# Seven half products in place of eight in the second feed-forward of a hybrid encoder

## The chip, the cores and the metric

The kernel runs on one core of one Trainium2 chip. The metric is the device time of one launch in microseconds (us); the comparison of two kernels uses medians of several runs on the same chip. Engines are named as the profile names them: PE is TensorE (matmuls), PEld the weight loads of TensorE, DVE is VectorE, ACT is ScalarE, POOL is GpSimd and SP issues the DMAs.

## What is computed

The reference is a two-layer encoder trunk on 512 tokens of width 1024, in float32. Each layer is a feed-forward, a mixer of four head groups, and a second feed-forward, each with an RMS norm before it. Only the second feed-forward is changed:

```
def rms_norm(x, gain):
    y = x * rsqrt(mean(x * x, axis=-1) + 1e-6)
    return y * gain

def swiglu(x, w_in, w_out):                 # w_in: 1024 x 5632, w_out: 2816 x 1024
    gate, up = split(x @ w_in, 2, axis=-1)
    return (silu(gate) * up) @ w_out

for layer in range(2):
    x = x + 0.5 * swiglu(rms_norm(x, ffn1_norm[layer]), ffn1_w_in[layer], ffn1_w_out[layer])
    x = x + hybrid_mixer(rms_norm(x, mix_norm[layer]), ...)
    x = x + 0.5 * swiglu(rms_norm(x, ffn2_norm[layer]), ffn2_w_in[layer], ffn2_w_out[layer])
```

## The kernel before

**Layout.** Everything is held transposed: x is eight tiles of 128 features by 512 tokens (x[0] to x[7]). Float32 products are formed from two parts of each operand in the type fp32r: the high part is the operand cast to fp32r, the low part is what the cast left. `mm3` (L106 to L109) issues three matmuls for one 128x128 weight block: low weight by high token (L107), high by low (L108), high by high (L109). The token operand (`norm_chunk`, L178) is x times the norm's gain, split into hh (ACT, L185) and hl (DVE, L186); the reciprocal root of the mean square, R, comes later from `norm_square` (L189; ACT squares, POOL adds, L196) and `stats` (L198), and is multiplied in behind the product.

**Weights.** `load` (L111) fetches a block of up to 128x1024 into one of two wr buffers by a DMA on SP's queue. `weights` (L116) cuts it into pieces of up to 512 columns and splits each: the cast to wh on ACT (L125), the subtraction to wl on DVE (L126). There are four wh and four wl buffers.

**The feed-forward** (`ffn`, L215). The 2816 hidden features are 22 chunks of 128, taken in four quarters of 6, 6, 5 and 5 chunks (`QS`). A chunk f loads its gate block and its up block (128x1024 each), and forms two products into two PSUM banks, pgp and pup: 8 blocks x 3 matmuls of 512 tokens each, 48 matmuls a chunk. Behind them come: gate by R (DVE, L250), Silu (ACT, L251), again by R (DVE, L252), up by gate (DVE, L254), and the split of the result (ACT, L256; DVE, L257) into `a`, of which a quarter keeps all its chunks. In chunk 0 the two products advance block by block as the norm's pieces arrive, and `stats` follows. After a quarter's chunks, `part` (L265) multiplies by the output weights: for each of 8 feature blocks d, n chunks x 3 matmuls of 512 tokens into pop (the first two blocks begin with all chunks but the last); then x[d] gets half of it added (DVE, L280), and in the last quarter the next norm's pieces are made.

**Order.** Nothing is ordered by hand here. The framework puts the instructions of each engine into one fixed order from the order in which the program writes them (earlier is more urgent), its own estimates of durations and the buffers that are free: 15 tiles of the tag t2 (128x512), 14 of k4 (128x1024), 5 of s8 (128x2048), 8 PSUM banks (three mm, two sc, two tp, one ot). At run time each engine takes its instructions in that order and waits on semaphores.

## Time and profile before

| what | us |
|---|---|
| median of 3 runs (lowest to highest) | 2024.93 (2024.31 to 2025.15) |
| the profiled execution's own time | 2025.69 |
| span in its profile, first to last instruction | 2023.9 |
| PE busy | 1969.1 |
| DVE busy | 1240.6 |
| ACT busy | 804.4 |
| POOL busy | 368.4 |

The profile's page has busy times, the chain of work that ended last (followed back from the last instruction to what released each step), groups of instructions by line, and DMA issues. The trace answers questions on a stretch of the span: busy time of each engine in it, who waited for whom, and the instructions in order of time. A matmul's recorded duration includes its way through the array, and matmuls overlap; what one costs in a row of them is the distance of their starts. The same holds, by less, on DVE and ACT. Layer 0's second feed-forward lies from about 648 us (its first matmuls run among the mixer's last) to 1025 us, layer 1's from about 1652 us to the end.

### The profile page before, as it was taken

The page shows a single profiled execution, that of the slowest core. Times are in us where ns is not written, and L with a number is a line of the kernel's source. Part 1 is how long each engine was busy: PE and PEld are TensorE (multiplying, and loading weights), DVE is VectorE, ACT ScalarE, POOL GpSimd, SP SyncE. Part 2 cuts the span into 40 slices and gives each one's busy share as a digit, 9 for nine tenths or more (in the row PEclk, how much of TensorE's full clock was granted, in tenths as well). Part 3 has the DMA queues.
Part 4 walks back from the last instruction along what each step waited for, and adds up shares of the span by engine and source line. Part 5 has one row for each costly group of instructions (what it writes and reads, how often), then busy time and mean ns, then how long its engine had stood idle before and what let it go on. Part 6 is the DMA issues. An engine that isn't in the chain of part 4 may idle for free.

```text
span 2023.9 us, 26161 instructions
## 1 busy us (share of the span) xinstructions
PE 1969.1 (97%) x9768; PEld 1648.9 (81%) x9768; DVE 1240.6 (61%) x2327; ACT 804.4 (40%) x1523; POOL 368.4 (18%) x349
## 2 busy tenths in 40 slices
PE   8999999998999999999999999999989989999999
PEld 6788878897977788888888888888978778888887
DVE  6865547657887545444577655465687875444454
ACT  4333323444676323233442333334547653232332
POOL 4010100254445000000120101002544540000000
PEclk9999999998999999999999999999989999999999
DMA  5232343331312332323233332423313122333233
GB/s 176 82 104 88 104 83 106 97 114 51 97 55 72 97 101 91 97 89 109 84 116 88 102 93 93 102 88 103 119 39 99 50 66 94 99 96 103 81 107 104
DMA packets 74447, 189.24 MB, mean 93 GB/s; under 512 B 16960, under 2 KB 22848, under 8 KB 74320
## 3 DMA queue, kind: packets, MB, share of 16 engines
q1 hardware_dynamic: 74224, 187.51, 30.7%
q8 instruction: 76, 1.25, 0.3%
q14 instruction: 51, 0.42, 0.1%
q0 software_dynamic: 96, 0.07, 0.0%
HBM read 182.86 MB, written 4.69 MB: 93 GB/s over the span
## 4 chain that ended last, share of the span: by engine, by line
PE 83%; DVE 10%; ACT 4%; issue 2%; POOL 1%; DMA 0%; SPq 0%; DVEq 0%; ACTq 0%; POOLq 0%
PE pop L109 9%; PE pop L108 9%; PE pop L107 9%; PE pup L107 7%; PE pgp L107 7%; PE pgp L108 7%; PE pgp L109 7%; PE pup L109 7%; PE pup L108 7%; PE ppr L107 1%; PE ppr L108 1%; PE ppr L109 1%; DVE wl L126 1%; PE pfp L448 1%; DVE hl L186 1%
## 5 line engine op out<-in xcount | busy, mean ns | idle before, releaser
L125 ACT CAST wh<-wr 128x512 fp32r<-128x512 f32 (+2 forms) x718 | 405.9, 570 | 962.8 <-PE pgp L109 314.0
L126 DVE TENSOR_TENSOR wl<-wr,wh 128x512 fp32r<-128x512 f32 (+2 forms) x618 | 409.4, 665 | 380.0 <-ACT wh L125 378.3
L107 PE MATMUL pgp<-hh,wl 128*128 128x512 f32 x704 | 275.5, 391 | 7.6 <-DVE wl L126 7.6
L107 PE MATMUL pup<-hh,wl 128*128 128x512 f32 x704 | 276.3, 392 | 3.2 <-DVE wl L126 3.2
L107 PE MATMUL pop<-a,wl 128*128 128x512 f32 x704 | 277.0, 395 | 1.4 <-DVE wl L126 1.4
L108 PE MATMUL pgp<-hl,wh 128*128 128x512 f32 x704 | 275.5, 391 | 2.4 <-DVE hl L186 2.4
L109 PE MATMUL pop<-a,wh 128*128 128x512 f32 x704 | 276.3, 392 | 0.0
L108 PE MATMUL pop<-a,wh 128*128 128x512 f32 x704 | 274.5, 390 | 0.6 <-DVE a L257 0.6
L108 PE MATMUL pup<-hl,wh 128*128 128x512 f32 x704 | 275.0, 391 | 0.0
L109 PE MATMUL pup<-hh,wh 128*128 128x512 f32 x704 | 275.0, 391 | 0.0
L109 PE MATMUL pgp<-hh,wh 128*128 128x512 f32 x704 | 274.7, 390 | 0.0
L196 POOL TENSOR_TENSOR t<-t,sq 128x512 f32<-128x512 f32 x42 | 60.0, 1430 | 664.9 <-ACT sq L195 663.6
L107 PEld LDWEIGHTS pgp<-hh,wl 128*128 128x128 f32 x704 | 132.6, 188 | 35.7 <-DVE wl L126 8.0
L126 POOL TENSOR_TENSOR wl<-wr,wh 128x512 fp32r<-128x512 f32 (+1 forms) x100 | 131.2, 1317 | 161.7 <-ACT wh L125 125.4
L107 PEld LDWEIGHTS pup<-hh,wl 128*128 128x128 f32 x704 | 132.5, 188 | 33.6 <-DVE wl L126 5.6
L108 PEld LDWEIGHTS pgp<-hl,wh 128*128 128x128 f32 x704 | 132.6, 188 | 32.9 <-DVE hl L186 5.5
L109 PEld LDWEIGHTS pop<-a,wh 128*128 128x128 f32 x704 | 132.2, 188 | 30.6
L108 PEld LDWEIGHTS pop<-a,wh 128*128 128x128 f32 x704 | 132.2, 188 | 30.2 <-DVE a L257 1.0
L107 PEld LDWEIGHTS pop<-a,wl 128*128 128x128 f32 x704 | 132.3, 188 | 28.9 <-DVE wl L126 2.1
L109 PEld LDWEIGHTS pup<-hh,wh 128*128 128x128 f32 x704 | 132.4, 188 | 27.6
L109 PEld LDWEIGHTS pgp<-hh,wh 128*128 128x128 f32 x704 | 132.4, 188 | 27.6
L108 PEld LDWEIGHTS pup<-hl,wh 128*128 128x128 f32 x704 | 132.5, 188 | 27.4
(263 smaller groups left out, 3071.3 us busy)
## 6 DMA issues: line engine op xcount, KB each, us to landing
wr<-in_f_w SPq DMA_DIRECT2D x176, 512.0 KB, 3.4
wr<-in_f_w SPq DMA_DIRECT2D x64, 384.0 KB, 3.1
wr<-in_f_w SPq DMA_DIRECT2D x64, 320.0 KB, 2.9
wr<-in_wm SPq DMA_DIRECT2D x36, 512.0 KB, 3.5
bias<-in_ctab SPq DMA_DIRECT2D x8, 448.0 KB, 3.4
bias<-in_rbx SPq DMA_DIRECT2D x8, 448.0 KB, 3.8
wr<-in_woC SPq DMA_DIRECT2D x8, 384.0 KB, 3.1
x<-in_xt SPq DMA_DIRECT2D x8, 256.0 KB, 6.4
```

The costliest lines, as they stand in the source:

```text
L107: nc.tensor.matmul(out, ll, rh, start=start, stop=False)
L108: nc.tensor.matmul(out, lh, rl, start=False, stop=False)
L109: nc.tensor.matmul(out, lh, rh, start=False, stop=stop)
L125: nc.scalar.copy(hi[:, :w], r)
L126: (nc.gpsimd if pooled else nc.vector).tensor_tensor(lo[:, :w], r, f32(hi[:, :w]), op=ALU.subtract)
L186: stt(hl, x[c], gcol, f32(hh), op0=ALU.mult, op1=ALU.subtract)
L196: gtt(acc, acc, sq, op=ALU.add)
L448: nc.tensor.matmul(pt[r0:r0 + 64, c0 + 16:c0 + 144], bm[q][:, g].rearrange("p a c -> p (a c)"), v[q][:, g].rearrange("p j c -> p (j c)"), ...
```

## The change

The second feed-forward of both layers is called with `fast=True`; in it, chunks 1 to 21 take a new path, chunk 0 the old one. Of each chunk the gate weights (ga) and the up weights (ua) are cut into two halves of the input features, and the tokens into two halves of 256 (HT); the 2x2 product of halves is then formed from seven products of a half weight (128 outputs by 512 inputs) with a half token set, each 4 blocks x 3 matmuls of 256 tokens (`product`), 84 matmuls a chunk.

- **Weights:** four sums of weight halves, s1 to s4, are formed on POOL; then seven operands (a11, s1, a12, a22, s2, s4, s3) are each split by `split` (ACT cast, DVE subtraction, 512 columns). ga still goes through `load`; ua is loaded into a k4 tile.
- **Tokens:** `token_forms` makes, once per call, four combinations of token halves for each of the four pairs of feature tiles: two products with the gain on ACT, two differences of 256 columns on POOL, two on DVE, then a split of 1024 columns (ACT cast, DVE subtraction) into an s8 tile kept for the whole call.
- **Results:** products are gathered in the banks px, pz, py and pv; ACT copies four halves of 256 columns out of PSUM (c1, c2), DVE adds four halves of 256 columns, one input in PSUM, into g (gate) and u (up).
- **Order:** the seventh product (s3, `finish`) and all that follows it are put off: `close` of a chunk is issued in the middle of the next chunk, after its second product; that of a quarter's last chunk between the output products' first two parts. In `close` the second multiplication by R is on POOL.

```diff
--- before.py
+++ after.py
@@ -212,16 +212,115 @@
         nc.scalar.copy(R, rp)
         return R, rc, ms
 
-    def ffn(l, which, next_norm, hooks):
+    def split(src):
+        hi = pool.tile([P, 512], F32R, tag="wh", bufs=4, name=nm("wh"))
+        lo = pool.tile([P, 512], F32R, tag="wl", bufs=4, name=nm("wl"))
+        nc.scalar.copy(hi, src)
+        tt(lo, src, f32(hi), op=ALU.subtract)
+        return hi, lo
+
+    HT = S // 2
+
+    def token_forms(idx):
+        out = []
+        for kp in range(KC // 2):
+            ha, hb = t2(name="ha"), t2(name="hb")
+            act(ha, x[kp], AF.Copy, scale=gains[:, idx, kp:kp + 1])
+            act(hb, x[kp + 4], AF.Copy, scale=gains[:, idx, kp + 4:kp + 5])
+            s = k4([P, 4, HT], name="tsum")
+            gtt(s[:, 0], ha[:, HT:], ha[:, :HT], op=ALU.subtract)
+            gtt(s[:, 2], hb[:, HT:], ha[:, HT:], op=ALU.subtract)
+            tt(s[:, 1], hb[:, HT:], s[:, 0], op=ALU.subtract)
+            tt(s[:, 3], hb[:, :HT], s[:, 1], op=ALU.subtract)
+            tf = s8([P, 2, 4, HT], F32R, name="tf")
+            nc.scalar.copy(tf[:, 0], s)
+            tt(tf[:, 1], s, f32(tf[:, 0]), op=ALU.subtract)
+            out.append(tf)
+        return out
+
+    def product(out, w, right, first, last):
+        for kp in range(KC // 2):
+            lhs = [a[:, kp * P:(kp + 1) * P] for a in w]
+            rh, rl = right(kp)
+            nc.tensor.matmul(out, lhs[1], rh, start=first and kp == 0, stop=False, skip_group_check=True)
+            nc.tensor.matmul(out, lhs[0], rl, start=False, stop=False, skip_group_check=True)
+            nc.tensor.matmul(out, lhs[0], rh, start=False, stop=last and kp == KC // 2 - 1, skip_group_check=True)
+
+    def ffn(l, which, next_norm, hooks, fast=False):
         w1 = t["f%d_w1" % which]
         w2 = t["f%d_w2" % which]
+        forms = []
+
+        def part_of(half, lo):
+            return lambda kp: (h[kp + 4 * half][0][:, lo:lo + HT], h[kp + 4 * half][1][:, lo:lo + HT])
+
+        def form(i):
+            return lambda kp: (forms[kp][:, 0, i], forms[kp][:, 1, i])
+
+        def begin(f, before):
+            ga = load(w1[l, f, 0], 1024)
+            ua = k4([P, 1024], name="ua")
+            nc.sync.dma_start(ua, w1[l, f, 1])
+            a11, a12, a21, a22 = ga[:, :512], ga[:, 512:], ua[:, :512], ua[:, 512:]
+            s1, s2, s3, s4 = t2(name="s1"), t2(name="s2"), t2(name="s3"), t2(name="s4")
+            gtt(s1, a21, a22, op=ALU.add)
+            gtt(s2, s1, a11, op=ALU.subtract)
+            gtt(s4, a12, s2, op=ALU.subtract)
+            gtt(s3, a11, a21, op=ALU.subtract)
+            px, pz = bank("sc", name="px"), bank("tp", name="pz")
+            product(px[:, :HT], split(a11), part_of(0, 0), True, True)
+            c1, c2 = t2(name="c1"), t2(name="c2")
+            nc.scalar.copy(c1[:, :HT], px[:, :HT])
+            product(pz[:, :HT], split(s1), form(0), True, True)
+            nc.scalar.copy(c2[:, :HT], pz[:, :HT])
+            if before is not None:
+                before()
+            py = bank("mm", name="py")
+            product(py[:, :HT], split(a12), part_of(1, 0), True, True)
+            pv = bank("mm", name="pv")
+            product(pv[:, :HT], split(a22), form(3), True, True)
+            g, u = t2(name="g"), t2(name="u")
+            tt(g[:, :HT], c1[:, :HT], py[:, :HT], op=ALU.add)
+            nc.scalar.copy(c2[:, HT:], pv[:, :HT])
+            product(px[:, :HT], split(s2), form(1), False, True)
+            nc.scalar.copy(c1[:, HT:], px[:, :HT])
+            product(pz[:, :HT], split(s4), part_of(1, HT), False, True)
+            tt(g[:, HT:], c1[:, HT:], pz[:, :HT], op=ALU.add)
+
+            def finish():
+                product(px[:, :HT], split(s3), form(2), False, True)
+                tt(u[:, :HT], px[:, :HT], c2[:, HT:], op=ALU.add)
+                tt(u[:, HT:], px[:, :HT], c2[:, :HT], op=ALU.add)
+
+            return g, u, finish
         if l == 0 and which == 1:
             norm_chunk(0, 0)
         h = state["h"]
+        norm_idx = 3 * l + (0 if which == 1 else 2)
         R = None
         for qi, (f0, f1) in enumerate(QS):
             av = []
+            pend = None
+
+            def close(g, u, finish):
+                finish()
+                tt(g, g, R, op=ALU.mult)
+                act(g, g, AF.Silu)
+                gtt(g, g, R, op=ALU.mult)
+                af = t2(name="af")
+                tt(af, u, g, op=ALU.mult)
+                a = k4([P, 2, S], F32R, name="a")
+                nc.scalar.copy(a[:, 0], af)
+                tt(a[:, 1], af, f32(a[:, 0]), op=ALU.subtract)
+                av.append(a)
+
             for f in range(f0, f1):
+                if fast and f >= 1:
+                    if not forms:
+                        forms += token_forms(norm_idx)
+                    before = None if pend is None else (lambda p=pend: close(*p))
+                    pend = begin(f, before)
+                    continue
                 pre = early if f == 0 else []
                 gw = weights(w1[l, f, 0], 1024, raw=pre.pop(0) if pre else None)
                 uw = weights(w1[l, f, 1], 1024, raw=pre.pop(0) if pre else None)
@@ -270,6 +369,8 @@
                     mm3(ops[d], *ws[d](i * P), av[i][:, 0], av[i][:, 1], i == 0, i == n - 1)
 
             part(0, range(n - 1))
+            if pend is not None:
+                close(*pend)
             part(1, range(n - 1))
             for d in range(KC):
                 if d < 2:
@@ -944,7 +1045,7 @@
             for _ in hooks:
                 pass
         mixer(l, T, 3 * l + 2)
-        ffn(l, 2, 3 * l + 3 if l + 1 < DEPTH else None, None)
+        ffn(l, 2, 3 * l + 3 if l + 1 < DEPTH else None, None, True)
 
 
 def _tables():
```

## Rows read from the trace of the kernel before

**Rows 1.** page, busy time of the engines and the chain that ended last

```profile
PE 1969.1 (97%) x9768; PEld 1648.9 (81%) x9768; DVE 1240.6 (61%) x2327; ACT 804.4 (40%) x1523; POOL 368.4 (18%) x349
...
PE 83%; DVE 10%; ACT 4%; issue 2%; POOL 1%; DMA 0%; SPq 0%; DVEq 0%; ACTq 0%; POOLq 0%
```

**Rows 2.** windows over layer 0's second feed-forward, columns in the first row

```profile
core 0: us, PE busy (x) PEld busy (x) DVE busy (x) ACT busy (x) POOL busy (x), PEclk, DMA share, GB/s
...
668.00:1025.00 357.00, 357.00 (x1574) 294.55 (x1574) 181.82 (x279) 122.36 (x212) 10.14 (x8) 1.00 0.31 96
690.00:721.00 31.00, 31.00 (x139) 25.66 (x138) 14.74 (x23) 9.83 (x17) 0.00 (x0) 1.00 0.29 90
721.00:754.00 33.00, 33.00 (x146) 27.07 (x145) 14.78 (x25) 9.16 (x17) 0.00 (x0) 1.00 0.35 102
```

**Rows 3.** waits in 668 to 1025 us (total us, times, longest)

```profile
DVE wl L126 <- ACT wh L125: 96.2, 75, 2.9
...
ACT wh L125 <- PE pgp L109: 74.5, 40, 2.9
```

**Rows 4.** DVE timeline (start us, us, instruction): after two up products

```profile
688.84 0.69 DVE L254 TENSOR_TENSOR af<-pup,sg 128x512 f32<-128x512 f32 x1 [1.39 <-PE pup L109]
...
699.72 0.69 DVE L254 TENSOR_TENSOR af<-pup,sg 128x512 f32<-128x512 f32 x1 [1.39 <-PE pup L109]
```

**Rows 5.** PE timeline in the mixer, first and last of 19 matmuls

```profile
460.22 0.28 PE L109 MATMUL ppr<-wh,hh 128*128 128x256 f32 x1
...
462.38 0.28 PE L109 MATMUL ppr<-wh,hh 128*128 128x256 f32 x1
```

**Rows 6.** DVE timeline, two operations back to back

```profile
680.53 0.68 DVE L257 TENSOR_TENSOR a<-af,a 128x512 fp32r<-128x512 f32 x1
...
681.13 0.68 DVE L252 TENSOR_TENSOR sg<-sg,R 128x512 f32<-128x512 f32 x1
```

**Rows 7.** groups by form, all of the span: busy us, mean ns, idle before

```profile
L815 POOL TENSOR_TENSOR zi<-zi,rot 128x512 f32<-128x512 f32 x4 | 5.2, 1292 | 9.2 <-DVE zi L812 9.2
...
L716 DVE TENSOR_TENSOR pT<-ptp,pT 128x256 fp32r<-128x256 f32 x32 | 12.5, 416 | 3.0 <-ACT pT L715 3.0
...
L405 DVE TENSOR_TENSOR k<-k,k 128x1024 f32<-128x1024 f32 x4 | 4.9, 1215 | 0.0
...
L125 ACT CAST wh<-wr 128x512 fp32r<-128x512 f32 x446 | 275.0, 620 | 621.2 <-PE pgp L109 254.1 <-PE pup L109 225.3 <-PE pop L109 76.0
```

**Rows 8.** POOL and DVE timelines at a norm's square, both idle before

```profile
1013.75 1.29 POOL L196 TENSOR_TENSOR t<-t,sq 128x512 f32<-128x512 f32 x1 [2.44 <-ACT sq L195]
...
1014.14 1.45 DVE L126 TENSOR_TENSOR wl<-wr,wh 128x512 fp32r<-128x512 f32 x1 [0.28 <-ACT wh L125]
1015.51 0.68 DVE L280 SCALAR_TENSOR_TENSOR x<-pop,x 128x512 f32<-128x512 f32 x1
```

**Rows 9.** POOL and DVE timelines where both have work queued

```profile
650.85 9.93 POOL L196 TENSOR_TENSOR t<-t,sq 128x512 f32<-128x512 f32 x6 [0.42 <-ACT sq L195]
...
654.32 1.27 DVE L759 TENSOR_TENSOR x<-pop,x 128x512 f32<-128x512 f32 x2
...
655.52 4.13 DVE L186 SCALAR_TENSOR_TENSOR hl<-x,gains,hh 128x512 fp32r<-128x512 f32 x3
```

**Rows 10.** DVE and PE timelines early in layer 0's second feed-forward

```profile
662.59 1.28 DVE L126 TENSOR_TENSOR wl<-wr,wh 128x512 fp32r<-128x512 f32 x2
...
668.47 0.49 PE L108 MATMUL pgp<-hl,wh 128*128 128x512 f32 x1
```

**Rows 11.** PE timeline and windows after an idle stretch in the mixer

```profile
491.90 0.69 PE L849 MATMUL pyp<-zi,s 128*128 128x64 f32 x2 [5.67 <-DVE zi L837]
...
495.00:500.00 5.00, 5.00 (x25) 4.92 (x25) 2.23 (x4) 2.55 (x5) 0.00 (x0) 0.50 0.00 0
500.00:505.00 5.00, 5.00 (x25) 5.00 (x24) 2.03 (x3) 3.07 (x5) 0.00 (x0) 0.50 0.00 0
505.00:510.00 5.00, 5.00 (x43) 5.00 (x42) 4.52 (x12) 3.47 (x9) 1.31 (x1) 0.95 0.02 3
```


## The prediction

> **What bounds the kernel now.** I read the busy times and the chain that ended last first: TensorE is busy 97% of the span and holds 83% of the chain, VectorE 61% of the span, GpSimd 18% [rows 1]. But the change acts in one stage, so I read the windows over that stage: in layer 0's second feed-forward PE is busy 357.00 of 357 us at the full granted clock (1.00), DVE 181.82, GpSimd 10.14 and, between the norms, 0.00 [rows 2]. The waits of the stage say the same: ScalarE waits for matmuls to free a weight buffer, VectorE for ScalarE, and neither holds PE up [rows 3]. So the stage is a row of matmuls, and its price is their number by the distance of their starts. Two successive chunks end their up product 699.72 - 688.84 = 10.88 us apart [rows 4]: 48 matmuls of 512 tokens, 0.227 us each.
>
> **What the change takes from PE.** 42 chunks (21 in each of two layers) get 84 matmuls of 256 tokens in place of 48 of 512. The mixer has such a row: 18 distances in 462.38 - 460.22 = 2.16 us, 0.120 us each, every one with a weight block of its own [rows 5]. A chunk then costs 84 x 0.120 = 10.08 us, and PE saves 0.80 x 42 = 33.6 us. That is 7%, not an eighth: 0.120 is more than half of 0.227, because part of a matmul's price does not shrink with its tokens. The Trainium skill ("TensorE: Matmul & The Clock Gate", Back-to-back issue gap) gives N/2.4 + 2.5 ns for a lone matmul, 109 and 216 ns here; by it a chunk would save some 1.2 us and the change 50 us, an estimate that the rows, with 120 and 227 ns, do not bear out.
>
> **What it adds elsewhere.** A chunk's work off PE, with the distance of two DVE operations of 512 columns, 681.13 - 680.53 = 0.60 us [rows 6], and the durations of [rows 7]:
> - POOL: four sums of weight halves and one multiplication by R, five of 512 columns at 1.29 us alone, 6.5 us; before it had none here.
> - DVE, both inputs in SBUF: seven weight subtractions in place of four, g by R, u by g, the low part of a: 10 x 0.60 = 6.0 us.
> - DVE, one input in PSUM: four sums of 256 columns, at most 0.42 us each (the price of such a one), 1.7 us.
> - ACT: seven casts at 0.62, Silu and the cast of a at about the same, and four half-width copies at no more: under 8.1 us of 10.08, hidden beside PE. If it were not, a late cast would hold its product up.
> - DMA: the same bytes in as many transfers on SP's queue; ua goes to a k4 tile, so the wr pair turns over half as often. I cost it at nothing; DMA's share is 0.29 in the chunks now [rows 2].
>
> Each of these sums is under 10.08 us, so PE would stay the bound if they ran side by side. They do not. Where POOL adds a square and DVE meets a subtraction with both inputs in SBUF, that subtraction takes 1.45 us and ends after the POOL operation [rows 8], against 0.68 [rows 6]. Where both queues are full, six POOL operations take 9.93 us, 1.655 each, and the DVE operations beside them 4.13/3 = 1.38 each; two DVE operations that read a PSUM bank, issued in the same stretch, take 1.27 together, undisturbed [rows 9]. So the two take turns, a POOL operation keeping DVE out for about 1.655 - 0.60 = 1.05 us. One chunk then needs 5 x 1.05 + 6.0 = 11.25 us of turns, plus the PSUM sums where they don't fall into POOL's turns: between 0 and 1.7, and I take a quarter of it, 0.4, because POOL's pairs fill about three quarters of the time (5 x 1.655 of 11.25). **11.65 us a chunk**, 11.25 to 12.9, against 10.08 on PE and 10.88 before. While it lasts, this makes a chunk slower, by 0.77.
>
> **What covers it.** The excess of 1.57 us falls only on a chunk in which the one before is closed and the next one's sums are made. A quarter's first chunk closes none, its last prepares none, and the output products (33 us with DVE busy 14.78 and POOL idle [rows 2]) let the next quarter begin with four operands split: three products ahead of PE, 3 x 12 x 0.120 = 4.3 us.
> - Quarter of six: 4 x 1.57 - 4.3 = 2.0 us of stall. Quarters of five: 3 x 1.57 - 4.3 = 0.4 each.
> - First quarter: chunk 1 also needs the token forms. For four pairs that is 2 POOL differences (half of 1.05 each), 2 DVE differences (0.42) and a DVE subtraction of 1024 columns (1.22): 4 x 3.11 = 12.4 us of turns, with chunk 1's four sums (4.2) and two splits (1.2) 17.8 us. DVE is free for it at 662.59 + 1.28 = 663.9, PE begins chunk 1 at 668.47 [rows 10] and can do three products (4.3 us) without the last form, to 672.8. If all 17.8 come first, PE waits until 681.7, 8.9 us; if POOL's part hides wholly, 4 x 2.06 + 1.2 = 9.4 us end at 673.3 and it waits 0.5. I take 6, nearer the upper end, because [rows 9] shows the two queues interlocked in just this stretch. Then chunks 2 to 4 with a lead of two products: 3 x 1.57 - 2.9 = 1.8.
> - The close of a quarter's last chunk (two PSUM sums, three operations of 0.6 to 0.7 on DVE, ACT, DVE: some 2.6 us) lies under 12 to 15 output matmuls of 0.227: 2.7 to 3.4 us. Nothing, with no room to spare.
>
> **Sum.** Per layer 6 + 1.8 + 2.0 + 0.4 + 0.4 = 10.6 us of stall, 21.2 in all: 33.6 - 21.2 = 12.4 us gained. The profiled execution took 2025.69 by itself (span 2023.9), 0.8 above the median; 2025.69 - 12.4 = 2013.3, and against the median **2012.5 us**.
>
> **Rivals.**
> - **The turns bind in every chunk** (slower). Place: DVE's queue in chunks 1 to 21. DVE's order is fixed and POOL takes its turn whenever its next tiles are free, so the lead of three products may be gone at once and never come back. It decides if products wait for wl from a quarter's second chunk on. Price: (11.65 - 10.88) x 42 = 32 us and 12 for the forms: 2024.9 + 44 = 2069; with half of it 2047, with 12.9 a chunk some 2120. For it: [rows 8, 9]. Against it: the tiles for the next chunk's sums come free only as operands are split, which holds POOL back. The Trainium skill has this as a rule ("SBUF — State Buffer", Who interferes with whom): a VectorE instruction with two SBUF inputs and a GpSimd one that reads SBUF exclude each other for the whole instruction. The trace agrees that one waits; taken strictly with 1.29 and 0.60 it would be 12.45 us a chunk, where six turns show 1.655 us and not 1.89 a pair. Chance 0.27.
> - **The forms cost the clock** (about no change). An idle stretch of 5.67 us in the mixer was followed by matmuls at a granted clock of 0.50, the 1.2 GHz level, until about 505 us [rows 11], some 13 us, half of them lost. If chunk 1 waits that long in one piece, each layer loses some 6.5 more: 2012.5 + 13 = 2026, 2019 to 2035. Against it: the forms come in four pieces, with matmuls between. Chance 0.25.
> - **All cover holds**: forms done within chunk 0, no excess: 2024.9 - 33.6 + 3 = 1994. It asks that POOL and DVE meet seldom; [rows 9] speaks against that. Chance 0.07.
> - That matmuls of 256 tokens don't save what they should (0.130 each would end it: 84 x 0.130 = 10.9) I leave out; [rows 5] has the same shape with new weights each time.
>
> **How the numbers follow.** The forecast has 0.41 (2001 to 2021). No change means within 0.2%, 4 us, about what a measurement of this kernel can tell: 2020.9 to 2029. Faster: 0.41 + 0.07 + 0.02 of the clock case = 0.50. Same: 0.15 of the clock case. Slower: 0.08 of the clock case and 0.27 = 0.35. The low end, 1999, leaves out nearly all of the cover case; the high end, 2056, the upper half of the first rival. Faster cases hold half, with a range of their own of 1994 to 2020.
>
> **What would show it.** PE: 84 matmuls of 256 tokens at 0.120 where nothing stalls. DVE over 85% busy in the chunks; POOL's sums at about 1.7 us instead of 1.29; DVE subtractions at about 1.4 beside them. PE idle for wl by a few us in chunk 1 of each layer, by one or two in the later chunks of a quarter, hardly in the last. It is wrong if such waits come in every chunk (first rival), if the granted clock falls in chunk 1 (second), or if chunks of 10.1 us follow each other from the start (third).

## The result and the profile after

The changed kernel takes **2130.81 us** (2127.08 to 2139.25, four runs) where the kernel before takes 2025.04 on the same chip: a ratio of 1.0528, interval 1.0497 to 1.056. It is 106 us slower. The forecast was 2012.5, and even the range, which ended at 2056, missed it. The profiled execution below is the longest of the four (2139.25 us, span 2137.5).

The page after, busy times, chain, and two of the costliest groups:

```profile
PE 1980.6 (93%) x11280; PEld 1731.8 (81%) x11280; DVE 1504.2 (70%) x2603; ACT 937.5 (44%) x1841; POOL 713.3 (33%) x575
...
PE 74%; DVE 17%; ACT 4%; issue 4%; POOL 1%; DMA 0%; SPq 0%; DVEq 0%; ACTq 0%; POOLq 0%
...
L219 DVE TENSOR_TENSOR wl<-s,wh 128x512 fp32r<-128x512 f32 x168 | 179.7, 1081 | 49.0 <-ACT wh L218 48.9
...
L245 PE MATMUL ppz<-tf,wl 128*128 128x256 f32 x168 | 59.0, 351 | 96.0 <-DVE wl L219 96.0
```

Against [rows 1], PE has fallen from 97% to 93% of a longer span, and DVE's share of the chain has risen from 10% to 17%. PE now stands idle 96 us ahead of one group of matmuls, those of the second product (bank pz, left operand s1), and each time VectorE's subtraction for s1 is what it waits for. The subtractions for the four sums take 1.081 us each on the mean, where operations of the same size took 0.68 [rows 6].

The windows over layer 0's second feed-forward (columns: stretch, length, busy time and count of PE, PEld, DVE, ACT and POOL, granted PE clock, DMA share, GB/s), with the stretch of chunk 1 in pieces:

```profile
668.00:1060.00 392.00, 343.07 (x2243) 319.11 (x2242) 298.22 (x399) 180.21 (x355) 174.99 (x115) 0.92 0.26 80
665.00:670.00 5.00, 2.24 (x15) 1.71 (x14) 0.85 (x2) 1.58 (x2) 1.03 (x1) 0.76 0.36 148
670.00:675.00 5.00, 2.69 (x12) 2.40 (x12) 3.96 (x5) 4.99 (x9) 3.38 (x5) 0.50 0.00 0
...
690.00:695.00 5.00, 2.82 (x13) 2.82 (x14) 5.00 (x5) 0.00 (x0) 3.27 (x2) 0.50 0.03 4
695.00:700.00 5.00, 5.00 (x32) 5.00 (x32) 1.82 (x4) 2.04 (x5) 0.00 (x0) 0.67 0.30 104
```

Where [rows 2] had PE busy 357 of 357 us at clock 1.00, it is now busy 343 of 392 at 0.92. Two separate losses show: one long hole in chunk 1 with the clock at 0.50 (the 1.2 GHz level) on both sides of it, and many small ones later. The waits of the stage name three causes (total us, times, longest; the last row is of the queue on which SP issues DMAs):

```profile
POOL s L266 <- DMA ua<-in_f_w: 78.6, 16, 7.0
...
PE ppz L245 <- DVE wl L219: 47.4, 14, 19.5
...
ACT R L212 <- PE prp L210: 10.8, 1, 10.8
```

```profile
SPq L113 <- DVE wl L219: 259.3, 21, 31.5
...
SPq L263 <- PE ppx L247: 0.3, 1, 0.3
```

**Chunk 1.** The timelines of ACT, POOL, DVE and PE there, in this order (start, us, instruction, idle before it and what ended it):

```profile
668.40 0.58 ACT L212 COPY R<-prp 128x512 f32<-128x512 f32 x1 [10.76 <-PE prp L210]
...
670.83 0.71 ACT L228 ACTIVATE ha<-x,gains 128x512 f32<-128x512 f32 x1
...
671.62 0.73 POOL L231 TENSOR_TENSOR tsum<-ha 128x256 f32<-128x256 f32 x1 [4.28 <-ACT ha L228]
...
683.73 6.72 DVE L237 TENSOR_TENSOR tf<-tsum,tf 128x1024 fp32r<-128x1024 f32 x3
690.38 1.74 DVE L219 TENSOR_TENSOR wl<-s,wh 128x512 fp32r<-128x512 f32 x1
...
692.18 0.58 PE L245 MATMUL ppz<-tf,wl 128*128 128x256 f32 x1 [19.49 <-DVE wl L219]
```

ACT stood idle for 10.76 us although the forms' inputs were there: its queue held the copy of R first, and R waits for the statistics. So the forms began at 670.8 and not at 663.9. From then on VectorE and GpSimd were in each other's way; a 1024-column subtraction took 6.72/3 = 2.24 us (1.215 in [rows 7]), and all four stood in VectorE's queue ahead of s1's subtraction, for which the second product waits.

PE's row, before and then after, shows smaller losses on both sides of the hole (pst is the bank of the statistics' first matmuls, for the mean squares; a second group spreads what R is copied from):

```profile
665.39 0.39 PE L107 MATMUL pgp<-hh,wl 128*128 128x512 f32 x1
...
667.66 0.95 PE L203 MATMUL pst<-ones,t 128*128 128x2 f32 x8
```

```profile
665.09 0.95 PE L203 MATMUL pst<-ones,t 128*128 128x2 f32 x8
...
669.76 0.58 PE L245 MATMUL ppx<-hh,wl 128*128 128x256 f32 x1 [1.40 <-DVE sg L349]
...
698.32 0.29 PE L246 MATMUL ppv<-tf,wh 128*128 128x256 f32 x1
```

Before, chunk 1's gate product started at 665.39 us, and its matmuls filled PE's time around the statistics, whose two groups of matmuls took PE 0.81 and 0.35 us by the distance of starts. In the change chunk 1's first product needs a bank that comes free only behind R, and 669.76 - 665.09 = 4.67 us pass from the statistics to it: 3.5 us more. When it starts, the matmuls run at half clock already: its eleven distances, to 672.28 us, take 2.52 us, 1.2 more than at 0.119 (a chunk of e10, below, divided by 84). The hole is 19.90 us from start to start, 19.8 more than one distance, and the 28 distances behind it, up to 698.32 us, take 6.14 us, 2.8 more. Together chunk 1 loses 27.3 us here, 4.0 of them by the clock.

**The later chunks.** SP, POOL, DVE and PE around the second product of one chunk:

```profile
718.16 0.33 SPq L113 DMA_DIRECT2D wr<-in_f_w  x1
718.54 0.43 SPq L263 DMA_DIRECT2D ua<-in_f_w  x1
731.62 0.33 SPq L113 DMA_DIRECT2D wr<-in_f_w  x1
...
723.25 1.31 POOL L266 TENSOR_TENSOR s<-ua 128x512 f32<-128x512 f32 x1 [6.31 <-DMA ua<-in_f_w]
...
729.79 1.77 DVE L219 TENSOR_TENSOR wl<-wr,wh 128x512 fp32r<-128x512 f32 x1
...
728.22 0.39 PE L245 MATMUL ppz<-tf,wl 128*128 128x256 f32 x1 [1.89 <-DVE wl L219]
741.54 0.38 PE L245 MATMUL ppz<-tf,wl 128*128 128x256 f32 x1 [1.55 <-DVE wl L219]
```

This is a loop. SP issues a gate load into a wr buffer as soon as VectorE has subtracted the gate half that stood there (729.79 + 1.77 = 731.56, issue at 731.62), and the up load ua only behind it. ua lands 4.7 us after its issue (718.54 to 723.25), POOL forms s1 from it, ACT casts it, VectorE subtracts, PE runs, and VectorE's next subtraction of a gate half frees the next buffer. These two chunks follow each other 741.54 - 728.22 = 13.32 us apart, where the kernel before had 10.88 [rows 4].

### The profile page after: what moved, and what is told of

It reads as the page before. It is cut to its first block, busy times and chain, and to the rows that moved or that the text cites. A ratio compares the mean times of both kernels' runs of the same rounds, so it can differ in the third digit from the quotient of the medians.

```text
span 2137.5 us, 30236 instructions
## 1 busy us (share of the span) xinstructions
PE 1980.6 (93%) x11280; PEld 1731.8 (81%) x11280; DVE 1504.2 (70%) x2603; ACT 937.5 (44%) x1841; POOL 713.3 (33%) x575
## 3 DMA queue, kind: packets, MB, share of 16 engines
q8 instruction: 88, 1.44, 0.3%
## 4 chain that ended last, share of the span: by engine, by line
PE 74%; DVE 17%; ACT 4%; issue 4%; POOL 1%; DMA 0%; SPq 0%; DVEq 0%; ACTq 0%; POOLq 0%
PE pop L108 8%; PE pop L109 8%; PE pop L107 8%; DVE wl L219 3%; PE pup L107 3%; PE pgp L107 3%; PE pgp L109 3%; PE pgp L108 3%; PE pup L108 3%; PE pup L109 3%; PE ppz L245 2%; PE ppx L245 2%; PE ppx L246 2%; PE ppx L247 2%; PE ppz L247 2%
## 5 line engine op out<-in xcount | busy, mean ns | idle before, releaser
L219 DVE TENSOR_TENSOR wl<-s,wh 128x512 fp32r<-128x512 f32 x168 | 179.7, 1081 | 49.0 <-ACT wh L218 48.9
L107 PE MATMUL pgp<-hh,wl 128*128 128x512 f32 x368 | 144.6, 393 | 7.9 <-DVE wl L126 7.8
L107 PE MATMUL pup<-hh,wl 128*128 128x512 f32 x368 | 145.7, 396 | 3.4 <-DVE wl L126 3.4
L108 PE MATMUL pgp<-hl,wh 128*128 128x512 f32 x368 | 144.8, 393 | 2.4 <-DVE hl L186 2.4
L108 PE MATMUL pup<-hl,wh 128*128 128x512 f32 x368 | 144.3, 392 | 0.0
L109 PE MATMUL pup<-hh,wh 128*128 128x512 f32 x368 | 144.1, 392 | 0.0
L109 PE MATMUL pgp<-hh,wh 128*128 128x512 f32 x368 | 144.0, 391 | 0.0
L107 PE MATMUL ppr<-wh,hl 128*128 128x256 f32 x448 | 127.8, 289 | 1.4 <-ACT q L666 1.4
L108 PE MATMUL ppr<-wl,hh 128*128 128x256 f32 x448 | 127.8, 286 | 0.7 <-POOL wl L126 0.7
L109 PE MATMUL ppr<-wh,hh 128*128 128x256 f32 x448 | 127.6, 286 | 0.0
```

Source lines behind the costliest of these rows:

```text
L107: nc.tensor.matmul(out, ll, rh, start=start, stop=False)
L108: nc.tensor.matmul(out, lh, rl, start=False, stop=False)
L109: nc.tensor.matmul(out, lh, rh, start=False, stop=stop)
L219: tt(lo, src, f32(hi), op=ALU.subtract)
```

## The experiments

Line numbers move by a few with each edit. Each edit is made to the changed kernel alone, unless other edits are named with it. The runs come in three groups, e1 to e4, e5 to e8 and e9 to e12, each with the kernel before measured beside it (2026.04, 2025.13 and 2024.75 us); ratios are to that, and a microsecond of difference between groups says nothing. Distances of chunks are taken inside a quarter.

**e1: load ua one chunk earlier.** The up load of a chunk is issued with the gate load of the chunk before, so that it is there when the sums are due.

```diff
+        ups = {}
...
         def begin(f, before):
+            for j in (f, f + 1):
+                if j not in ups and j < NF:
+                    ups[j] = k4([P, 1024], name="ua")
+                    nc.sync.dma_start(ups[j], w1[l, j, 1])
             ga = load(w1[l, f, 0], 1024)
-            ua = k4([P, 1024], name="ua")
-            nc.sync.dma_start(ua, w1[l, f, 1])
+            ua = ups.pop(f)
+            ups.setdefault(f, None)
```

> Only the load of the up weights (ua) moves: each is issued one chunk earlier in the program, the result is the same. In the changed kernel's trace ua of a chunk is issued behind the gate load of the chunk after it, which waits for a wr buffer until a12 is subtracted; POOL waits 78.6 us for ua in layer 0's second feed-forward, and PE about 2.1 us at the second product of 14 of its 21 new chunks, which come 12.4 to 14 us apart. Theory A (the order of the loads): POOL's waits for ua fall under 20 us, chunks come about 11.65 us apart, what POOL's and DVE's turns allow; 28 chunks x 1.5 us = 42 us less than the changed kernel's 2130.8: 2089, 2075 to 2100. Theory B (the turns alone set the pace, the load is late only because all is late): within 10 us of 2130.8.

Measured: 2087.63 (2086.45 to 2089.33), ratio 1.0305 (1.029 to 1.032), 43 us less than the change. POOL no longer waits for ua, and the later chunks of a quarter are some 12.16 us apart (the first two distances of a quarter are 9.98 and 11.18). The load's place in the queue, and the sum that reads ua:

```profile
716.75 0.42 SPq L265 DMA_DIRECT2D ua<-in_f_w  x1
...
728.96 0.39 SPq L265 DMA_DIRECT2D ua<-in_f_w  x1
...
731.08 1.78 POOL L271 TENSOR_TENSOR s<-ua 128x512 f32<-128x512 f32 x1
```

ua is still issued right behind a gate load that waits (issued at 728.54, ua at 728.96), but it is now that of a later chunk: the sum at 731.08 reads the one issued at 716.75, 14.3 us before. VectorE's timeline of a chunk, beside POOL's:

```profile
721.16 1.78 DVE L316 TENSOR_TENSOR af<-u,g 128x512 f32<-128x512 f32 x1
722.86 0.41 DVE L288 TENSOR_TENSOR g<-c,ppy 128x256 f32<-128x256 f32 x1
723.19 1.44 DVE L219 TENSOR_TENSOR wl<-wr,wh 128x512 fp32r<-128x512 f32 x1
724.55 1.78 DVE L319 TENSOR_TENSOR a<-af,a 128x512 fp32r<-128x512 f32 x1
```

```profile
718.91 1.77 POOL L271 TENSOR_TENSOR s<-ua 128x512 f32<-128x512 f32 x1
...
722.47 1.61 POOL L273 TENSOR_TENSOR s<-wr,s 128x512 f32<-128x512 f32 x1
```

So the late load cost 43 us, and the turns of the two engines are what remains in the steady chunks: POOL's sums take 1.61 to 1.77 us, VectorE's operations with two inputs in SBUF up to 1.78, and the one that reads a PSUM bank 0.41 as ever. The wait in chunk 1 is the same as in the change (19.4 us).

**e2: no token forms** (the token halves themselves stand in for them; this part of the computation is missing).

```diff
         def form(i):
-            return lambda kp: (forms[kp][:, 0, i], forms[kp][:, 1, i])
+            return part_of(i % 2, HT * (i // 2))
...
-                    if not forms:
-                        forms += token_forms(norm_idx)
```

> Left out: the token forms (ACT, POOL, DVE); the four products that read them read plain token halves instead. Both theories on the chunks leave the rest as it is. If the forms made the long wait in chunk 1 (PE idle 19.5 us at its second product, then matmuls at half the granted clock until about 698 us, in all some 27 us a layer), this gives 55 us less: 2076, 2065 to 2090. Rival: chunk 1 waits for the norm's R, which holds the PSUM bank that px takes, and for weights all the same; then at most 25 us less: 2105 or more.

Measured: 2103.11 (2100.95 and 2105.26), ratio 1.0381 (1.036 to 1.0401), 27.7 us less than the change, where 55 were forecast. Chunk 1 still waits, 1.40 us at the first and 3.80 at the second product, and the later chunks wait for ua as before (74.3 us in the stage, against 78.6). The forms cost about 14 us a layer in the changed kernel as it stands.

**e3: no sums of weights** (the raw halves are used in their place; this part is missing).

```diff
-            s1, s2, s3, s4 = t2(name="s1"), t2(name="s2"), t2(name="s3"), t2(name="s4")
-            gtt(s1, a21, a22, op=ALU.add)
-            gtt(s2, s1, a11, op=ALU.subtract)
-            gtt(s4, a12, s2, op=ALU.subtract)
-            gtt(s3, a11, a21, op=ALU.subtract)
+            s1, s2, s3, s4 = a21, a11, a22, a12
```

> Left out: the four sums of weight halves on POOL; the products that read them read plain weight halves. Multiplying by R stays on POOL. Theory B (turns): DVE's subtractions fall from 1.08 to about 0.7 us, chunks to 10.1 to 10.5 us, 28 x 2.5 = 70 us less: 2061, 2050 to 2075. Theory A (order of the loads): ua is still issued late, but its way to the product is shorter by a POOL sum and its blocked followers, some 4 us; so chunks near 10.1 to 11 too, 2060 to 2085, with ScalarE or DVE now waiting for ua's DMA. It bounds what the sums cost in all, and does not by itself tell A from B.

Measured: 2053.25 (2052.66 and 2053.85), ratio 1.0135 (1.0114 to 1.0155), 77.6 us less than the change. The later chunks of a quarter are 10.7 to 11.4 us apart and PE still waits some 1 us in each: now ACT waits for ua (24.1 us in the stage). Even without sums the late load costs 30 us (against e5, below).

**e4: the sums on VectorE**, POOL keeping the multiplication by R (four times `gtt` to `tt` in the lines of e3).

> The four sums move from POOL to DVE, the result is the same; the order of the loads stays. DVE then has 14 operations with both inputs in SBUF (8.4 us), four PSUM sums (1.4 to 1.7) and one turn of POOL (1.05): about 10.8 us a chunk, with almost no turns to wait for. Theory B (turns): chunks come 10.8 to 11 us apart, 28 x 2 = 56 us less: 2075, 2065 to 2090. Theory A (order of the loads): the loop of a12's subtraction, load, sum, cast and subtraction still sets the pace, shorter by about 1 us for the sum and 1 to 2 us for unblocked subtractions: 2085 to 2110, with PE still waiting at the second product.

Measured: 2091.58 (2090.87 to 2093.24), ratio 1.0325 (1.0308 to 1.0342). The later chunks of a quarter are 12.66 us apart, the wait in chunk 1 is 13.16 us. It is nearly e1's time by another way: four sums at VectorE's own 0.60 cost it less than standing aside for POOL's. ua is still issued late, behind a gate load, but VectorE waits for it only 1.3 us in the stage; it waits 17.4 us there for the product in pz, and one subtraction a chunk takes 1.76 us beside POOL's multiplication by R. Which of these holds the pace at 12.66 is not shown.

**e5: e1 and e3 together** (the sums are missing here too).

> Left out: the four sums of weight halves on POOL, as in the run without sums; and ua's load is issued one chunk earlier, as in the first run. That run's chunks came 12.16 us apart, those without sums about 11.1, with ScalarE waiting 24.1 us for ua's DMA. If the order of the loads and the turns are the two causes and nothing else holds the chunks, both are gone here and chunks come 10.1 to 10.3 us apart, PE's own pace: 2087.6 - 28 x 1.95 = 2033, less some 8 us for each layer's chunk 1: 2017, 2005 to 2028. Rival C (a third limit: DVE's and ScalarE's fixed order with only four weight buffers of half the former cover): chunks stay near 11 us, 2035 or more.

Measured: 2023.23 (2022.04 to 2025.52, ten runs), ratio 0.9991 (0.9982 to 1.0001): no change that can be told. The windows of the steady chunks and the one wait that is left:

```profile
685.00:690.00 5.00, 5.00 (x28) 5.00 (x27) 2.56 (x5) 1.33 (x3) 0.00 (x0) 0.57 0.01 3
...
700.00:740.00 40.00, 40.00 (x317) 39.02 (x316) 31.62 (x56) 23.59 (x48) 5.19 (x4) 1.00 0.34 103
```

```profile
683.57 0.58 PE L245 MATMUL ppz<-tf,wl 128*128 128x256 f32 x1 [10.82 <-DVE wl L219]
```

After chunk 1 PE never waits, yet the kernel gains nothing: the hole of 10.82 us in chunk 1, with matmuls at clock 0.50 before it and 0.57 after it, and the time lost around the statistics, as in the change, use up what twenty chunks save.

**e6: forms ahead of the statistics, px and pz from alternating banks.** The forms then stand in ACT's queue ahead of R's copy, and a chunk's first product need not wait for the bank that chunk 0's gate product holds until R is there.

```diff
-            px, pz = bank("sc", name="px"), bank("tp", name="pz")
+            tag = "tp" if f % 2 else "sc"
+            px, pz = bank(tag, name="px"), bank(tag, name="pz")
...
-                    if not forms:
-                        forms += token_forms(norm_idx)
...
+                    if fast:
+                        forms += token_forms(norm_idx)
                     R, _, _ = stats()
```

> The result is the same; the order of the loads stays as in the changed kernel. Two edits for chunk 1: the token forms are issued before the statistics of the norm (in the changed kernel ScalarE's queue has them behind the copy of R, so they start at 670.8 us though ScalarE was idle from 657.6), and px and pz take both banks of one kind in turn, so that px of chunk 1 no longer waits for the bank that chunk 0's gate product holds until R. Theory: the long wait of chunk 1 is the queue order, not the forms' own work: 12 to 20 us a layer less, 2130.8 - 30 = 2100, 2088 to 2110. Rival: the forms' turns only move into chunk 0, where they hold up the norm's pieces; then less than 10 us in all, 2120 or more. The run without forms gave 27.7 us.

Measured: 2118.33 (2114.53 to 2120.79), ratio 1.0462 (1.0447 to 1.0478), 12.5 us less than the change, less than half of the 30 forecast. The wait falls from 19.49 to 13.08 us, and 2.31 us come ahead of the first product: an earlier place in the queue alone does not bring the forms in time.

**e7 and e8: e1 and e6 together, without most or all of POOL.** e7 leaves POOL the sums of the first two new chunks of a quarter and gives VectorE the rest and the second multiplication by R; e8 gives VectorE all of them.

```diff
+            add = gtt if f - max(f0, 1) < 2 else tt      # e7; in e8 tt throughout
-            gtt(s1, a21, a22, op=ALU.add)
+            add(s1, a21, a22, op=ALU.add)
...
-                gtt(g, g, R, op=ALU.mult)
+                tt(g, g, R, op=ALU.mult)
```

> A version meant to be faster, the result is the same: ua's load one chunk earlier, forms before the statistics, the banks in turn, and few turns: POOL makes the sums for the first two new chunks of a quarter (which fall beside the output products, where DVE has time), DVE those of the others, and DVE also the second multiplication by R. DVE then has 15 operations with both inputs in SBUF and four PSUM sums in a chunk, 10.4 to 10.7 us without turns, PE 10.08. Expected: chunks 10.4 to 10.9 us apart against 10.88 in the kernel before, so 0 to 20 us gained on them, and 5 to 12 us a layer lost in chunk 1: 2033, 2012 to 2050. If DVE's queue, full to 98%, brings waits of its own: 2050 to 2075.

> As the run before it, but all sums on DVE; POOL has only the forms' differences. It tells whether POOL's sums in the cover of the output products help: if they do, this is 5 to 15 us slower than that run, because each quarter's first chunks wait for sums on DVE; if DVE has room there, the same within 4 us.

Measured: e7 2046.65 (2045.74 to 2046.78), ratio 1.0109 (1.0092 to 1.0125); e8 2032.30 (2031.42 to 2033.34), ratio 1.0039 (1.0024 to 1.0054). That is the other way round than was expected: the sums that e7 leaves to POOL cost it 14 us, though VectorE in e8 is busy nearly all of the time. Two second products of e8, and the window over them:

```profile
711.76 0.39 PE L245 MATMUL ppz<-tf,wl 128*128 128x256 f32 x1 [0.36 <-DVE wl L219]
722.55 0.38 PE L245 MATMUL ppz<-tf,wl 128*128 128x256 f32 x1 [0.36 <-DVE wl L219]
```

```profile
700.00:720.00 20.00, 19.64 (x164) 19.31 (x164) 18.88 (x35) 11.66 (x24) 0.00 (x0) 1.00 0.32 100
```

These chunks are 10.79 us apart with VectorE busy 94% (the first three distances of a quarter 9.98 to 10.69), and its 512-column subtractions take 0.686 us each (mean of 168 for the sums' low parts), against 1.081 in the change. Chunk 1 still waits 8.42 us, 13.35 in e7: with layer 1's (8.7 and 13.2) that is 9.4 of the 14 us between the two.

**e9 to e12: the seven products begin with the third chunk** (`if fast and f >= 2`), so that chunk 1 goes the old way and the forms have its time too. All four have e1's and e6's edits. e9 has no work on POOL (as e8), e10 leaves out the sums of weights (that part is missing), e11 keeps the sums and the multiplication by R on POOL as the change has them, e12 is e9 with the two PSUM sums into u joined in one instruction.

> As e8_no_pool (sums, u and R on VectorE, load of ua one chunk earlier, forms ahead of the layer's statistics, px and pz from alternating banks), and the seven products begin only with the third chunk, so that the second chunk of each layer goes the old way with eight. Theory A (the stall at the layer's first new chunk is the forms coming too late, and with its half clock it eats the saving): with one more chunk to be made in, the forms are there, the stall of about 10 us a layer in chunk 1 and the half clock behind it go, and the time falls by 12 to 24 us under e8: 2008 to 2020, below the kernel before for the first time. Rival (VectorE is full at 10.78 us a chunk, and what waits in chunk 1 waits later): within 5 us of e8, 2027 to 2037.

> As e9, and the sums of the weights are left out as in e3 (so this part of the computation is missing), to see what the seven products alone give. If PE's share was priced right (40 chunks, 7 x 4 fewer... a saving of 0.80 us a chunk as forecast), 2025 - 40 x 0.8 = 1993, between 1988 and 2003. Rival (chunks are kept apart by the other engines even without the sums): 2010 to 2025.

> As e9, but with the sums on POOL and VectorE as the change has them. Theory A (turns of POOL and VectorE set 12.16 us a chunk as in e1, and the forms are out of the way): chunks 12.1 us apart where PE could go at 10.1 to 10.8, so some 1.4 us over e9 in each of 40 chunks: 2060 to 2080. Rival (the turns were a result of the late forms and of the loads): within 10 us of e9.

> As e9, with the two sums from PSUM that close the up product joined to one instruction of VectorE (px read twice by a broadcast). If VectorE sets the pace of the chunks, one fixed cost of an instruction a chunk is saved: 2 to 6 us less than e9 over 40 chunks. If PE sets it, the same within 2 us.

Measured, with the kernel before at 2024.75 (2023.31 to 2027.0, 21 runs) on the same chip:

| | us (lowest to highest) | ratio (interval) |
|---|---|---|
| e9, all on VectorE | 2021.78 (2019.99 to 2022.63) | 0.9985 (0.9977 to 0.9994) |
| e10, no sums | 2006.43 (2004.25 to 2006.69) | 0.9908 (0.9894 to 0.9921) |
| e11, sums on POOL | 2058.30 (2057.53 to 2059.44) | 1.0167 (1.0153 to 1.0181) |
| e12, joined sum | 2021.44 (2020.42 to 2022.95) | 0.9983 (0.9974 to 0.9992) |

e9's wait in chunk 2, and two later ones; then two of e11's; then two chunks of e10, one chunk lying between them, by the start of their third product:

```profile
686.46 0.58 PE L245 MATMUL ppz<-tf,wl 128*128 128x256 f32 x1 [3.37 <-DVE wl L219]
...
802.76 0.39 PE L245 MATMUL ppz<-tf,wl 128*128 128x256 f32 x1 [0.36 <-DVE wl L219]
813.54 0.38 PE L245 MATMUL ppz<-tf,wl 128*128 128x256 f32 x1 [0.36 <-DVE wl L219]
```

```profile
808.54 0.39 PE L245 MATMUL ppx<-hh,wl 128*128 128x256 f32 x1 [1.05 <-DVE wl L219]
...
820.70 0.39 PE L245 MATMUL ppx<-hh,wl 128*128 128x256 f32 x1 [1.04 <-DVE wl L219]
```

```profile
698.98 0.29 PE L245 MATMUL ppy<-hh,wl 128*128 128x256 f32 x1
...
718.95 0.29 PE L245 MATMUL ppy<-hh,wl 128*128 128x256 f32 x1
```

- e9 is 10.5 us under e8: most of the wait of chunk 1 is gone (3.37 us instead of 8.42), a little less than the 12 to 24 expected, because a wait is left and the granted clock is 0.66 in the 10 us around it. Chunk 2's wait is no longer one for the forms: VectorE makes s1 only at 684.29 us, when all four pieces of the forms are done (by 676.9). It is the first version that beats the kernel before, by 3 us.
- e10 shows what seven products are worth undisturbed: (718.95 - 698.98) / 2 = 9.99 us a chunk, 0.89 less than 10.88. Yet the kernel gains 18 us and not 40 x 0.89 = 36. Layer 0's stage ends at 1017.97 us, before at 1027.30 (the start of the next norm's statistics on PE): 9.3 earlier in place of 17.8, so 8.5 us a layer are lost. They are lost at the stage's head. The first output product starts 3.45 us later than before (724.67 against 721.22), although three new chunks and six of the seven products of a fourth come ahead of it, which should save 3 x 0.89 + 10.88 - 6/7 x 9.99 = 5.0: 8.4 us together. The rows below show where: chunk 1's first matmul starts 3.26 us after the statistics' (665.77 to 669.03; 0.81 before), because VectorE has the subtraction of chunk 1's gate weights in its queue behind operations for the forms; the second product of chunk 2 starts 2.5 us late, at 686.02, with a wait of 2.31 us for VectorE; and behind each of these two waits some matmuls run at half clock, by their distances 1.6 and 1.5 us longer than at full clock. That is 8.0 of the 8.4.

```profile
669.03 0.50 PE L107 MATMUL pgp<-hh,wl 128*128 128x512 f32 x1 [2.32 <-DVE wl L126]
```

```profile
667.50 0.87 DVE L233 TENSOR_TENSOR tsum<-hb,tsum 128x256 f32<-128x256 f32 x1
668.29 0.68 DVE L126 TENSOR_TENSOR wl<-wr,wh 128x512 fp32r<-128x512 f32 x1
```

- e11 is 36.5 us over e9 with the same products, loads and forms: POOL's part of the work alone, 12.16 us a chunk (820.70 - 808.54) against 10.78 in the later chunks of a quarter.
- e12 is the same as e9. VectorE is free 0.06 us earlier in a chunk, and waits as much longer for ACT's cast of the next piece (0.40 us instead of 0.34); the chunks stay 10.78 us apart. So a wait for ACT takes its part in the pace, and VectorE's busy time alone does not set it.

## Why the prediction was wrong

Step by step, with what stands in the place of each:

1. **PE's price was right**, slightly on the safe side: 9.99 us a chunk where nothing stalls (e10), forecast 10.08. The saving is 0.89 us a chunk and not 0.80, some 18.7 a layer. The trouble is all in what PE waits for.
2. **"DMA: the same bytes in as many transfers on SP's queue … I cost it at nothing" failed.** The bytes are the same and DMA's share is 0.26 in the stage; but a load's place in SP's queue was not counted. The up load stands behind a gate load that waits for a wr buffer, and the buffer comes free only when VectorE has split the chunk that depends on the load before. With that one load issued a chunk earlier the change takes 43 us less (e1), which shows what its lateness cost. That it is late because of its place is read from the trace: SP's waits for ua's own tile come to 0.3 us in the stage, those for the gate load's buffer ahead of it to 259.3. Neither a third wr buffer nor an up load ahead of its own gate load was tried. The prediction's argument, "the wr pair turns over half as often", holds for the buffers and says nothing of the load behind them. Why the gate load stands first in that queue (tiles of one tag are handed out in the order of the program) is argued from the order of issues in the trace, and was not tried by itself.
3. **"6 us" of waiting for the forms failed by its size, and the time around the statistics was put at nothing.** The wait for the forms measured 19.49 us. Four things had been taken too well. The start: 663.9 assumed, 670.83 measured, because ACT's queue had R's copy first. The lead: three products ahead of the last form assumed, one measured, because s1's subtraction stands behind all the forms' in VectorE's queue; and the second product, as the change is written, reads all four pieces of the forms. The duration: 17.8 us of turns, measured from the first form on ACT to the second product 692.18 - 670.83 = 21.4, in which POOL also made the sums of chunk 2. And chunk 1's begin: the prediction read 668.47 us from [rows 10], but that row lies in the middle of chunk 1's old gate product, which starts at 665.39 and hid the statistics; the new first product cannot, since it waits for a bank until R is there, and 3.5 us are lost.
4. **The clock rival's condition came true, at a lower price than it named.** From 670 to 695 us the granted clock is 0.50, the 1.2 GHz level, until 700 it is 0.67. By the distances of starts this costs some 4.0 us in layer 0 where the rival had 6.5 a layer, and 1.2 of them lie ahead of the hole: the clock falls from 665 to 670 us (0.76), where PE is busy 2.24 of 5 us around the statistics. Chunk 1 as a whole loses 3.5 + 19.8 + 4.0 = 27.3 us, an estimate from the distances, where 6 were forecast. e5 agrees: without sums its chunk 1 takes all that the later chunks save, about 18 us a layer (0.8 gained of 18.7 at the end of layer 0's stage, 1026.52 against 1027.30 us), and with the sums the hole is 19.49 - 10.82 = 8.7 us longer, some 27 again.
5. **The turns were sized too small and their cover much too large.** 11.65 us a chunk forecast, 12.16 measured in e1 and e11 (with 0.9 us in it in which VectorE waits for a cast); the pairs of [rows 9] at 1.655 us are POOL's sums at 1.61 to 1.77. That is near, but what counts is the excess over PE, 12.16 - 9.99 = 2.17 us where 1.57 was forecast. The prediction let it fall on 13 chunks of a layer, and so it does: 13 x 0.60 = 7.8 us more. What failed by more is the cover, "three products ahead of PE, 4.3 us" in each quarter and 2.9 in the first, 15.8 in all. The waits of e1's stage:

```profile
PE ppz L245 <- DVE wl L219: 27.4, 14, 19.4
...
PE ppx L245 <- DVE wl L219: 9.8, 9, 1.2
```

   In e1's second quarter the third products start at 785.01, 794.99, 806.17, 818.22, 830.48 and 842.66 us, distances of 9.98, 11.18, 12.05, 12.26 and 12.18: beyond the first, only the second is clearly shorter, by 1.0, and the other quarters look alike. So the cover is worth some 4.1 us a layer and not 15.8. By the distances the turns cost e1 24.1 us a layer where 1.8 + 2.0 + 0.4 + 0.4 = 4.6 were forecast; the waits show 17.8 of it, 27.4 - 19.4 = 8.0 at the second product beside chunk 1's and 9.8 at the first. That comes near the first rival, "the turns bind in every chunk", with 13 of 20 distances; that rival named 2069, and e11, whose forms and loads come mostly in time, has 2058.
6. The Trainium skill's rule that I set beside that rival ("SBUF — State Buffer", Who interferes with whom: two SBUF inputs on VectorE and a GpSimd instruction that reads SBUF exclude each other) is borne out in its direction by 0.686 us (e8, POOL idle) against 1.081 (the change), and by the 0.41 us of the operation that reads PSUM between two of 1.78 and 1.44.

The sum of layer 0: its stage ends at 1082.69 us after, at 1027.30 before, 55.4 later. PE's saving is -18.7 (21 x 0.89); chunk 1 costs about 27 (step 4); what is left, 47, lies in the other twenty chunks. e1's stage ends at 1059.66, with the same wait in chunk 1, so 23 of the 47 are the loads, and 24 are left to the turns, as the distances in e1 say too. (The profiled execution of the change lies 8 us above its median and that of e1 1 us, so the 23 are a little high: by the medians the loads are 43 us for both layers.) The same edits one after the other over the whole kernel: the change 2130.8; ua earlier 2087.6; forms earlier and a chunk later to be used 2058.3 (e11); nothing on POOL 2021.8 (e9); no sums at all 2006.4 (e10). So without the sums 18 us are gained, and the sums, on the engine that does them best here, take back 15 of those (e10 has the multiplication by R on POOL, e9 on VectorE).

What stays open: the clock's 4.0 us are worked out from distances, and no run has the clock without the wait; which of its waits holds e4 at 12.66 us; whether another place in the queue alone would bring ua in time; and whether the forms could be made early enough with the seven products from chunk 1 on.

## What to carry to other kernels

Before a saving on the bound engine is counted, follow each operand it needs backwards through the queues in their order: a load that stands behind another load's buffer wait, or a small piece of work that stands behind one which waits for something else, costs what the waiting one costs, though no engine is full. Work for two engines that exclude each other is to be added up, not set side by side; here moving four sums and a multiplication from the idler engine to the busier one made the kernel 36 us faster. A product that runs while something else is computed is cover, and is missed when it is replaced: chunk 1's old gate product hid 3.5 us of statistics. And a long stall of TensorE is paid twice: as idle time, and again as matmuls at half clock behind it (here 19.8 us and 2.8).

## What the runs showed that I had not expected

- A stall of 0.36 us in the records costs more than 0.36: in e9 the chunk with it is 10.78 us long, 0.79 more than e10's, though no other wait over 0.3 us stands in PE's row. The record of a matmul reaches over the start of the next (0.28 us at a distance of 0.12), so the idle time shown is the shorter part of the gap between the starts: 802.12 to 802.76 us, 0.64 in place of 0.12.
- VectorE's 1024-column subtraction takes 2.289 us on the mean of eight beside a busy POOL (the change) and 1.212 in e11, where POOL stands idle while layer 0's four run (670 to 677 us).
- The clock is given back late: in the change, the granted clock is 0.50 from 690 to 695 us and 0.67 until 700, with matmuls 0.21 us apart from 692.56 to 698.32, after a hole of 19.49 us; e9's wait of 3.37 us leaves 0.66 in the 10 us from 685 on.
